# Transposing the last quarter's probabilities and the first gated rows by DMA in a two-layer decoder trunk

## The chip, the cores and the metric

The kernel runs on one core of a Trainium2 chip. The metric is device time in microseconds (us) of one execution; the time before is the median of three runs. A profile of one execution gives every instruction on the five engines with its start and length. PE (TensorE) multiplies matrices and writes PSUM, with a weight loader, PEld, beside it; DVE (VectorE), ACT (ScalarE) and POOL (GpSimd) work elementwise; SP (SyncE) issues the DMA transfers. Each engine, and SP's queue too, takes its instructions in a fixed order, and each instruction waits at the head of its queue until what it reads is there and what it overwrites is free.

## What is computed

The input is 256 tokens of width 1024. Layer 0 is a dilated attention mixer and layer 1 a forgetting attention mixer; each is followed by a gated feed-forward layer. All values are float32. Cut to what matters here:

```python
def dilated_mixer(h, w_in, w_out):                 # 3 groups (dilation 1, 4, 16), 16 heads of 64
    proj = (h @ w_in).reshape(B, S, N_GROUPS, 3, N_HEADS, HEAD_DIM)
    for g, (window, dil) in enumerate(DILATED_PATTERNS):
        ...
        o, lse = dilated_band_attention(q, k, v, dil, window // dil)
    wts = jax.nn.softmax(jnp.stack(lses, axis=0), axis=0)
    o = jnp.einsum('gbsh,gbshd->bshd', wts, jnp.stack(outs, axis=0))
    return o.reshape(B, S, ATTN_WIDTH) @ w_out

def swiglu(h, w_gu, w_down):                       # D_FF = 2816
    gu = h @ w_gu
    g, u = gu[..., :D_FF], gu[..., D_FF:]
    return (jax.nn.silu(g) * u) @ w_down

for i in range(2):
    h = h + (dilated_mixer, forgetting_mixer)[i](rmsnorm(h, ...), ...)
    h = h + swiglu(rmsnorm(h, ffn_norm[i]), ffn_w_gu[i], ffn_w_down[i])
return rmsnorm(h, final_norm)
```

## The kernel before

**Products in three parts.** Every large product is computed with its operands cut into a high part and a low part (`split`, L76: ACT copies the high part, L80, and DVE subtracts to get the low part, L84). One product is then three matmuls (`mm3`, L200, lines L203 and L208): high by high, high by low, low by high. In this text an *item* is one such group of three with an output of 512 columns.

**Weights.** They arrive in pieces of 128x2048, listed in use order in `order` (L141 to L149). `weights` (L154) issues each piece's two loads from SP into `raw` (five buffers) and cuts them on ACT and DVE into `wh` and `wl` (four buffers each, one pair per piece), up to two pieces ahead of the one that is used. In the feed-forward layer of the kernel before, the order is gu0, gu1, gu2, gu3, dn0, gu4, dn1, gu5, gu6, dn2 and so on: "gu" holds the gate and up columns of 128 hidden units, "dn" the down rows of 256.

**Mixer of layer 0.** The 16 heads are worked in four quarters, `hq` 0 to 3, each with two pairs of heads, `pr` 0 and 1. The 36 units of `a_units` are projections; attention steps are put behind units with `later(i, ...)`. A pair's probabilities are 128x640 per head, and the product with the values (`pv_a`, L534) needs them transposed in blocks of 128x128. There are two ways to transpose:

- Quarters 0 to 2 use `turn_a` (L519). A float32 is taken as two 16-bit halves. POOL copies the halves apart (L528), a transposing DMA issued from SP turns all ten 128x128 blocks of 16-bit values (L530, tile `turned`), and ACT joins the halves again (L531). The tiles lie in tag `pt` (three buffers) and tag `bias` (four buffers).
- Quarter 3 uses `trans_a` (L510): ten transposes on PE per pair into PSUM (`transposed`, L297, line L301), and copies out of PSUM (L306). Due at 38 and 39, with `pv_a` at 40, these run inside `out_proj`.

`values_12` (L274) moves the values of the two dilated groups into place with 16 POOL copies (L285). For quarter 3 they stand in the next-to-last unit.

**`out_proj`** (L658) multiplies the attention output `ot` (eight slices `k` of 128; slices 6 and 7 are the last quarter's) with four weight pieces, for token halves t = 0, 1 and column halves n = 0, 1. In layer 0 it does six items of t = 0 (n = 0, slices 0 to 5), the transposes of pair 0, three items, the transposes of pair 1, three items, `pv_a` for both pairs, and then the four items with slices 6 and 7. For t = 1 it does four items, then eight with `norm_t` of token half 0 behind them (L185: two normalisation passes on DVE, eight PE transposes at L196), and four more.

**Feed-forward layer** (`ffn`, L702). The first three gu pieces are computed in token-major layout, so that work can start before both token halves are normalised: gu0 and gu1 as a pair (`proj_pair`), gu2 by `proj_tok`. `gated` (L711) takes Silu on ACT (L714) and the product on DVE (L715). The results must be transposed before `down` can use them: four PE transposes for gu0 and gu1 (L775), two for gu2 (L784), each followed by `split` from PSUM. From gu3 on, `up` (L718) computes feature-major and needs no transposes; it uses one PSUM bank of tag `mm` (gate) and one of tag `tr` (up). `down(j, t)` (L733) adds piece dn j's product for token half t. The order is up(3), down(0), up(4), down(1), up(5), up(6), down(2) and so on. In layer 0 the result of gu2 itself lies in an `mm` bank, in layer 1 in an `o` bank. There are two banks per tag.

**Order of work.** The program text gives priorities; `first()` (L44) raises those of what it holds by 300, and `issue_after` ties an instruction behind another on its engine. The final order on each engine is fixed before the run.

Of the kernel before, what the change touches and what calls it, by code (L numbers as in the profile page):

```python
# [17 lines left out]
P = 128  # L18
# [14 lines left out]
def trunk(ctx: ExitStack, tc: tile.TileContext, T, out):  # L33
# [221 lines left out]

    def v_tile(o=None, r=None):

        v = ap.tile([P, 512], F32, tag="v", name="v", bufs=7)
        with first():
            if r:  # L260
                for t in range(2):
                    s = slice(t * S, (t + 1) * S)
                    nc.scalar.activation(v[:, s], o[:, s], AF.Copy, scale=r[t])
            elif o is not None:
                nc.scalar.activation(v, o, AF.Copy)
        return v
# [27 lines left out]

    copied = {}
# [214 lines left out]
    def trans_a(quad, pr):  # L510

        pt = quad["pt"]
        block = lambda h, i: pt[pr, h][:, i * P:(i + 1) * P]
        home = ("pt", "bias")[pr]
        quad["w", pr] = [transposed([block(h, 1 + qb) for h in range(2) for qb in range(2)], nc.scalar.copy, home=home),
                         transposed([block(h, 3) for h in range(2)], home=home),
                         transposed([block(h, b * 4) for h in range(2) for b in range(2)], nc.scalar.copy, "o", home)]

    def turn_a(quad, pr):  # L519

        quad["w", pr] = []
        bufs = {"pt": 3, "bias": 4}
        parts = lambda x: x[:, :640].bitcast(U16).rearrange("p (c t) -> p t c", t=2)
        for h in range(2):
            home = ("pt", "bias")[pr]
            w = ap.tile([P, 640 if home == "pt" else 6 * P], F32, tag=home, name="pt", bufs=bufs[home])
            split16 = w[:, :640].bitcast(U16)
            nc.gpsimd.tensor_copy(split16.rearrange("p (t c) -> p t c", t=2), parts(quad["pt"][pr, h]))  # L528
            turned = ap.tile([P, 6 * P], F32, tag="bias", name="turned", bufs=4)[:, :640].bitcast(U16)
            nc.sync.dma_start_transpose(turned.rearrange("p (g c) -> p g c", c=P), split16)  # L530
            nc.scalar.copy(parts(w), turned.rearrange("p (t c) -> p t c", t=2))  # L531
            quad["w", pr].append(w)

    def pv_a(quad, pr):  # L534
        vs, ws = quad["v"], quad["w", pr]
        o = psum("o")
        if len(ws) == 2:
            blocks = [w[:, :640].rearrange("p (i j) -> p i j", j=P) for w in ws]
            straight = lambda h: ws[h][:, P:3 * P]
            corner = lambda h: ws[h][:, 3 * P:4 * P]  # L540
            dilated = lambda h, a: blocks[h][:, 0:5:4, a * 32:a * 32 + 32]
        else:
            straight = lambda h: ws[0][:, h * S:(h + 1) * S]
            corner = lambda h: ws[1][:, h * P:(h + 1) * P]
            dilated = lambda h, a: halves(ws[2][:, h * S:(h + 1) * S], a)
        pv(o[:, :S], vs[0], 0, pr, straight, S, True, False)
        pv(o[:, P:S], vs[0], 1, pr, corner, P, False, False)
        halves = lambda x, a: x.rearrange("p (b n) -> p b n", b=2)[:, :, a * 32:a * 32 + 32]
        for a in range(4):
            pv(halves(o[:, :S], a), vs[1 + a % 2], a // 2, pr, lambda h: dilated(h, a), 64, False, a == 3)  # L550
# [6 lines left out]
    def later(i, fn, *a):  # L557
        due.setdefault(i, []).append((fn, a))

    quads = [{"hq": hq, "fm": {}, "pt": {}, "v": {}} for hq in range(4)]  # L560
    for i, (hq, g, w) in enumerate(a_units):
# [19 lines left out]
        if w < 2:  # L581
# [26 lines left out]
            if w == 1:  # L608
# [5 lines left out]
                if g == 2:  # L614
                    later(j + 1, scores_12, quad)
                    later(j + 1, softmax_a, quad)
                    for pr in range(2):
                        if hq == 3:
                            later(step(hq) + pr, trans_a, quad, pr)
                        else:  # L620
                            later(j + 1, turn_a, quad, pr)
# [36 lines left out]
    def out_proj(nm, ot, h, grow, ks, done, banks):  # L658
# [3 lines left out]
        res = []  # L662

        def part(t, acc, nk):
            last = None
            for n, k in nk:
                c = (k % 2) * D + n * 512
                last = mm3(acc[n], both(ot, ALL, k, slice(t * P, (t + 1) * P)),
# [3 lines left out]
        def cols(ks):  # L672
            return [(n, k) for n in range(2) for k in ks]

        for t in range(2):
            acc = [psum(banks[t]) for _ in range(2)]
            if t == 0:

                nk = cols(range(ks))
                last = part(t, acc, nk[:done])  # L680
                nk = nk[done:]
                per = -(-len(nk) // (len(due) - 1))
                for i in sorted(due):
                    with tc.issue_after(last.ins):
                        for fn, a in due[i]:
                            fn(*a)
                    last = part(t, acc, nk[:per]) or last
                    nk = nk[per:]
                due.clear()
                part(t, acc, nk)  # L690
                last = part(t, acc, cols(range(ks, KT)))
            else:
                part(t, acc, cols(range(2)))
                with tc.issue_after(last.ins):
                    part(t, acc, cols(range(2, 6)))
                    norm_t(*res[0], grow, xt, 0)
                    part(t, acc, cols(range(6, KT)))
            res.append(residual(acc, h[t], f"h_{nm}{t}"))
# [3 lines left out]
    def ffn(l, hs, xt, grow, mid):  # L702
# [54 lines left out]
        rows = {}  # L757
# [14 lines left out]
        tr = psum("tr")  # L772
        for f in range(2):
            for t in range(2):
                nc.tensor.transpose(tr[:, f * S + t * P:f * S + (t + 1) * P], rows[t][:, f, :], ident)  # L775
        act(0)
        split(acts[0], lambda y: y, tr)
# [4 lines left out]
        tr = psum("tr")  # L782
        for t in range(2):
            nc.tensor.transpose(tr[:, t * P:(t + 1) * P], a[:, t, :], ident)  # L784
# [26 lines left out]

    g_f = load_grow(1)
    hs, xt = out_proj("a_out", ot, x, g_f, 6, 6, ("sc", "mm"))
# [195 lines left out]
    hs, xt = out_proj("b_out", ot, [h for h, _ in hs], g_f, 6, 9, ("mm", "sc"))  # L1009
# [129 lines left out]
```

## Time and profile before

| | us |
|---|---|
| median of 3 runs | 737.42 (736.22 to 738.65) |
| the profiled execution's own time | 736.1 |
| its span, first to last instruction | 734.3 |
| around the span | 1.8 |
| weight and input bytes read | 136.00 MB, 187 GB/s over the span |
| granted TensorE clock, mean | 0.997 |

The page names busy time per engine, a picture of the span in 40 slices, the DMA queues, the chain of work that ended last, and the costliest groups of instructions. A matmul's listed length includes its pipeline, so that neighbours overlap: the time that one costs is the distance to the start of the next. Busy shares are means over stages with different limits; which wait counts is read from the timeline of a stage.

### The profile page before, as it was taken

How to read it: one execution, taken by the hardware profiler on the slowest of the kernel's cores; microseconds unless marked ns; L12 is line 12 of the kernel's file. 1: busy time of each engine (PE TensorE's matmuls, PEld its weight loads, DVE VectorE, ACT ScalarE, POOL GpSimd, SP SyncE). 2: the span in 40 equal slices, each digit the busy share in tenths (PEclk: the TensorE clock that was granted, in tenths of full speed). 3: DMA queues.
4: the chain of work that ended last, by engine and by line, in shares of the span. 5: the costliest groups of instructions: out<-in, count | busy, mean ns of one | idle time of the engine just before them, and what ended most of it. 6: DMA issues, size and time to landing. Idle time of an engine off the chain costs nothing.

```text
span 734.3 us, 14310 instructions
## 1 busy us (share of the span) xinstructions
PE 726.4 (99%) x5856; PEld 672.4 (92%) x5856; DVE 495.9 (68%) x762; ACT 388.7 (53%) x617; POOL 83.0 (11%) x118
## 2 busy tenths in 40 slices
PE   9999999999999999999999999999999999999996
PEld 7999989999988899999999989999889999999995
DVE  6997998998996775554555474576776554556533
ACT  7646747738445663444554453587475444545421
POOL 0600206007105000000000004110010000000001
PEclk9999999999999999999999999999999999999998
DMA  9865955956864376656567352874547656656601
GB/s 335 306 202 174 237 182 153 289 193 152 268 194 160 116 241 221 195 179 203 195 202 247 127 168 90 294 260 138 172 142 237 222 179 203 195 188 218 198 1 58
DMA packets 55042, 141.93 MB, mean 193 GB/s; under 512 B 20257, under 2 KB 21441, under 8 KB 54977
## 3 DMA queue, kind: packets, MB, share of 16 engines
q1 hardware_dynamic: 54832, 140.88, 59.4%
q8 instruction: 46, 0.75, 0.4%
q14 instruction: 20, 0.16, 0.1%
q10 hardware_dynamic: 144, 0.15, 0.1%
HBM read 136.00 MB, written 1.07 MB: 187 GB/s over the span
## 4 chain that ended last, share of the span: by engine, by line
PE 97%; DVE 1%; ACT 1%; POOL 0%; issue 0%; POOLq 0%; DVEq 0%; ACTq 0%
PE ps_mm L208 34%; PE ps_mm L203 17%; PE ps_tr L208 9%; PE ps_sc L208 8%; PE ps_o L208 7%; PE ps_tr L203 5%; PE ps_sc L203 4%; PE ps_o L203 4%; PE ps_o L313 2%; PE ps_sc L395 2%; PE ps_tr L196 1%; PE ps_tr L301 1%; PE ps_sc L476 1%; PE ps_o L322 1%; PE ps_sc L894 0%; PE ps_sc L458 0%
## 5 line engine op out<-in xcount | busy, mean ns | idle before, releaser
L80 ACT ACTIVATE wh<-raw 128x1024 fp32r<-128x1024 f32 x236 | 243.4, 1054 | 207.1 <-PE ps_tr L208 66.7
L84 DVE TENSOR_TENSOR wl<-raw,wh 128x1024 fp32r<-128x1024 f32 x236 | 288.3, 1242 | 82.6 <-ACT wh L80 82.4
L203 PE MATMUL ps_mm<-xt,wh 128*128 128x256 f32 x816 | 227.2, 279 | 0.2 <-ACT v L281 0.2
L208 PE MATMUL ps_mm<-xt,wl 128*128 128x256 f32 x816 | 226.0, 277 | 0.0
L208 PE MATMUL ps_mm<-xt,wh 128*128 128x256 f32 x816 | 226.0, 277 | 0.0
L203 PEld LDWEIGHTS ps_mm<-xt,wh 128*128 128x128 f32 x816 | 153.1, 188 | 2.2 <-issue 1.7
L208 PEld LDWEIGHTS ps_mm<-xt,wl 128*128 128x128 f32 x816 | 153.6, 188 | 0.1
L208 PEld LDWEIGHTS ps_mm<-xt,wh 128*128 128x128 f32 x816 | 153.4, 188 | 0.0
L208 PE MATMUL ps_tr<-xt,wh 128*128 128x256 f32 x304 | 83.9, 276 | 0.0
L208 PE MATMUL ps_tr<-xt,wl 128*128 128x256 f32 x304 | 83.9, 276 | 0.0
L203 PE MATMUL ps_tr<-xt,wh 128*128 128x256 f32 x304 | 83.7, 276 | 0.0
L730 DVE TENSOR_TENSOR sa<-ps_tr,sa 128x256 f32<-128x256 f32 x38 | 16.1, 424 | 73.5 <-PE ps_tr L208 73.5
L208 PEld LDWEIGHTS ps_tr<-xt,wh 128*128 128x128 f32 x304 | 57.1, 188 | 0.0
L208 PEld LDWEIGHTS ps_tr<-xt,wl 128*128 128x128 f32 x304 | 57.0, 188 | 0.0
L203 PEld LDWEIGHTS ps_tr<-xt,wh 128*128 128x128 f32 x304 | 57.0, 188 | 0.0
L203 PE MATMUL ps_mm<-wh,xt 128*128 128x512 f32 (+1 forms) x144 | 49.8, 346 | 0.0
L173 POOL TENSOR_SCALAR rs<-ssq 128x1 f32<-128x1 f32 x7 | 1.9, 271 | 420.6 <-ACT junk L182 420.6
L208 PE MATMUL ps_mm<-wl,xt 128*128 128x512 f32 (+1 forms) x149 | 49.1, 335 | 0.0
L208 PE MATMUL ps_mm<-wh,xt 128*128 128x512 f32 (+1 forms) x149 | 49.1, 335 | 0.0
L285 POOL COPY v<-v 32x256 f32<-32x256 f32 x64 | 40.5, 632 | 71.2 <-ACT v L281 68.6
L203 PE MATMUL ps_sc<-wh,ah 128*128 128x512 f32 x80 | 31.4, 392 | 0.0
L208 PE MATMUL ps_sc<-wl,ah 128*128 128x512 f32 (+1 forms) x82 | 31.3, 385 | 0.0
(232 smaller groups left out, 1113.6 us busy)
## 6 DMA issues: line engine op xcount, KB each, us to landing
raw<-in_gu SPq DMA_DIRECT2D x88, 512.0 KB, 4.8
raw<-in_a_in SPq DMA_DIRECT2D x68, 512.0 KB, 5.0
raw<-in_dn SPq DMA_DIRECT2D x44, 512.0 KB, 4.7
raw<-in_b_in SPq DMA_DIRECT2D x24, 512.0 KB, 5.0
raw<-in_a_out SPq DMA_DIRECT2D x8, 512.0 KB, 5.0
raw<-in_b_out SPq DMA_DIRECT2D x8, 512.0 KB, 4.4
bias<-sums SPq DMA_DIRECT2D x8, 384.0 KB, 6.6
grow<-in_norms SPq DMA_DIRECT2D x4, 512.0 KB, 5.7
```

The lines of the kernel that those rows point to most:

```text
L80: a = nc.scalar.activation(view(hi), src, AF.Copy)
L84: return nc.vector.tensor_tensor(view(lo), src, view(hi).bitcast(F32), op=ALU.subtract)
L196: nc.tensor.transpose(tr[:, k * P:(k + 1) * P], xn[:, kk * P:(kk + 1) * P], ident)
L203: nc.tensor.matmul(o, sh, mh, start=start, stop=False)
L208: last = nc.tensor.matmul(o[:, u], s, m[:, u], start=False, stop=end and u.stop == n)
L285: nc.gpsimd.tensor_copy(v[1 + a % 2][n:n + 32, a // 2 * S:a // 2 * S + S], by_t[a * 32:a * 32 + 32, t, g])
L301: nc.tensor.transpose(tr[:, i * P:(i + 1) * P], b, ident)
L313: nc.tensor.matmul(o[h * HD:(h + 1) * HD], v[:, c:c + HD], w(h), start=start, stop=stop)
L322: nc.tensor.matmul(o[:, :n], mhalf.to_broadcast([P, P]), mhalf.to_broadcast([P, n]), start=True, stop=True)
L395: nc.tensor.matmul(lead[t], xt[y][:, k, t * P:(t + 1) * P], w[z][:, u], start=k + y + z == 0, stop=k == KT - 1 and z == 1)
L476: nc.tensor.matmul(sc[h][c, o:o + 64], q[HR[h], pr, qb * P + a * 32:qb * P + a * 32 + 32], k[HR[h], pr].rearrange("p (b n) -> p b n", b=2) ...
L730: nc.vector.tensor_tensor(a, u, sg, op=ALU.mult)
```

## The change

- Quarter 3 uses `turn_a` too. Its 16-bit halves are copied apart on POOL for pair 0 and on DVE for pair 1, with raised priority. The joining copies are a function of their own, `join_a`, due at 38 (pair 0, on ACT, tied behind the last copy of the values) and at 39 (pair 1, on DVE). `trans_a` is gone.
- For pair 1, head 0, of every quarter the `turned` tile lies in tag `pt` and not in tag `bias`. In quarter 3 three `pt` and five `bias` tiles are used, with three and four buffers.
- `out_proj` takes a list of items `head` and places `at` which the due work stands. In layer 0 the list has 16 items: slices 0 to 3 of t = 0 (eight items), slices 0 and 1 of t = 1 (four), slices 4 and 5 of t = 0 (four). The joins stand behind items 4 and 9, `pv_a` behind item 16. The four items of t = 1 are therefore done before `pv_a`, and not after the residual of t = 0. In layer 1 the list and places give the order of before.
- In `ffn`, `gate` copies the halves of the gated rows apart (POOL for token half 0, DVE for token half 1); `turned` issues one transposing DMA and joins on ACT; `split` then reads SBUF. The third piece, gu2, goes the same way with POOL. The six PE transposes of each layer are gone.
- down(0) moves behind up(4), directly in front of down(1); the weight order becomes gu3, gu4, dn0, dn1, gu5.

```diff
-            order += [(f"gu{l}", f)] + ([(f"dn{l}", max(f // 2 - 1, 0))] if f == 3 or f % 2 == 0 and f > 3 else [])
+            order += [(f"gu{l}", f)] + [(f"dn{l}", 0)] * (f == 4) + [(f"dn{l}", f // 2 - 1)] * (f > 3 and f % 2 == 0)
...
-    def trans_a(quad, pr):
...
     def turn_a(quad, pr):
...
+        last = quad["hq"] == 3
+        by = (nc.gpsimd, nc.vector)[last and pr].tensor_copy
+        home = lambda tag: turn_tile(tag)[:, :640]
+        quad["w", pr], quad["turned", pr] = [], []
         for h in range(2):
...
+            with first() if last else nullcontext():
+                w = home(("pt", "bias")[pr])
+                apart = w.bitcast(U16)
+                by(apart.rearrange("p (t c) -> p t c", t=2), parted(quad["pt"][pr, h]))
+                turned = home(("bias", "pt")[pr * (h == 0)]).bitcast(U16)
+                nc.sync.dma_start_transpose(turned.rearrange("p (g c) -> p g c", c=P), apart)
             quad["w", pr].append(w)
+            quad["turned", pr].append(turned)
+            if not last:
+                join_a(quad, pr, h)
+
+    def join_a(quad, pr, h, by=nc.scalar.copy):
+        with tc.issue_after(copied["v"].ins) if quad["hq"] == 3 else nullcontext():
+            by(parted(quad["w", pr][h]), quad["turned", pr][h].rearrange("p (t c) -> p t c", t=2))
...
                     for pr in range(2):
-                        if hq == 3:
-                            later(step(hq) + pr, trans_a, quad, pr)
-                        else:
-                            later(j + 1, turn_a, quad, pr)
+                        later(j + 1, turn_a, quad, pr)
+                        for h in range(2) if hq == 3 else ():
+                            later(38 + pr, join_a, quad, pr, h, (nc.scalar.copy, nc.vector.tensor_copy)[pr])
...
+        cols = lambda t, ks: [(t, n, k) for n in range(2) for k in ks]
+        last = None
+        for a, b in zip((0, *at), (*at, len(head))):
+            last = part(head[a:b]) or last
+            if due:
+                with tc.issue_after(last.ins):
+                    for fn, a in due.pop(min(due)):
+                        fn(*a)
+        last = part(cols(0, range(KT)))
+        res = [residual(accs[0], h[0], f"h_{nm}0")]
+        part(cols(1, range(2)))
+        with tc.issue_after(last.ins):
+            part(cols(1, range(2, 6)))
+            norm_t(*res[0], grow, xt, 0)
+            part(cols(1, range(KT)))
+        res.append(residual(accs[1], h[1], f"h_{nm}1"))
...
+        rows = turn_tile("pt")[:, :512]
+        row16 = rows.bitcast(U16).rearrange("p (t f x c) -> p t f x c", t=2, f=2, x=2)
...
+        def turned(apart, by):
+            n = apart.shape[-1]
+            w = turn_tile("bias")[:, :n].bitcast(U16)
+            nc.sync.dma_start_transpose(w.rearrange("p (g c) -> p g c", c=P), apart.bitcast(U16))
+            by(parted(apart).rearrange("p x (f t c) -> p t f x c", t=2, c=P),
+               w.rearrange("p (t f x c) -> p t f x c", t=2, x=2, c=P))
 
         def gate(t):
             gu = pair[t].rearrange("p (a c b) -> p a c b", a=2, c=2)
-            rows[t] = gated(gu[:, :, 0, :], gu[:, :, 1, :], 2)
+            a = gated(gu[:, :, 0, :], gu[:, :, 1, :], 2)
+            with first():
+                (nc.gpsimd, nc.vector)[t].tensor_copy(row16[:, t], halves(a))
...
-        tr = psum("tr")
-        for f in range(2):
-            for t in range(2):
-                nc.tensor.transpose(tr[:, f * S + t * P:f * S + (t + 1) * P], rows[t][:, f, :], ident)
         act(0)
-        split(acts[0], lambda y: y, tr)
+        with first():
+            turned(rows, nc.scalar.copy)
+            split(acts[0], lambda y: y, rows)
         third = act(2)
         up(3)
         gu = o.rearrange("p (a c b) -> p a c b", a=2, c=2)
         a = gated(gu[:, :, 0, :], gu[:, :, 1, :], 2)
-        tr = psum("tr")
-        for t in range(2):
-            nc.tensor.transpose(tr[:, t * P:(t + 1) * P], a[:, t, :], ident)
-        split(*third, tr[:, :S])
-        for f in range(2, NF):
-            if f > 3:
-                up(f)
-            if f % 2 == 0:
-                j = f // 2 - 1
+        row = turn_tile("pt")[:, :S]
+        nc.gpsimd.tensor_copy(row.bitcast(U16).rearrange("p (t x c) -> p t x c", t=2, x=2), halves(a))
+        turned(row, nc.scalar.copy)
+        split(*third, row)
+        for f in range(4, NF):
+            up(f)
+            for j in {4: (0, 1)}.get(f, (f // 2 - 1,) if f % 2 == 0 else ()):
                 dn[j] = weights(f"dn{l}", j)
...
+    def blocks(t, ks):
+        return [(t, n, k) for i in ks for n in range(2) for k in (2 * i, 2 * i + 1)]
...
+    hs, xt = out_proj("a_out", ot, x, g_f, blocks(0, range(2)) + blocks(1, range(1)) + blocks(0, (2,)), (4, 9, 16),
+                      ("sc", "mm"))
...
+    hs, xt = out_proj("b_out", ot, [h for h, _ in hs], g_f, [(0, n, k) for n in range(2) for k in range(6)], (9, 12),
+                      ("mm", "sc"))
```

More of the change, by code (lines that the diff above doesn't have):

```diff
@@ L254, in p_tile @@
         return ap.tile([P, 640], dtype, tag="p", name=name, bufs=6)[:, :n]
+    copied = {}
     def v_tile(o=None, r=None):
@@ L508, in softmax_a, with parted @@
                         nc.vector.tensor_scalar(s, s, f, None, op0=ALU.mult)
-    def trans_a(quad, pr):
[L512 to L517, printed above, removed]
+    def parted(x):
+        return x.bitcast(U16).rearrange("p (c t) -> p t c", t=2)
@@ L519, in turn_a, with turn_tile @@
+    def turn_tile(tag):
+        return ap.tile([P, 640 if tag == "pt" else 6 * P], F32, tag=tag, name="pt", bufs={"pt": 3, "bias": 4}[tag])
     def turn_a(quad, pr):
-        quad["w", pr] = []
-        bufs = {"pt": 3, "bias": 4}
-        parts = lambda x: x[:, :640].bitcast(U16).rearrange("p (c t) -> p t c", t=2)
+        last = quad["hq"] == 3
+        by = (nc.gpsimd, nc.vector)[last and pr].tensor_copy
+        home = lambda tag: turn_tile(tag)[:, :640]
+        quad["w", pr], quad["turned", pr] = [], []
@@ L524, in turn_a @@
         for h in range(2):
[L525 to L530, printed above, removed]
@@ L536, in pv_a @@
         o = psum("o")
[L537 to L541, printed above, removed]
-        else:
[L543 to L547, printed above, removed]
+        blocks = [w.rearrange("p (i j) -> p i j", j=P) for w in ws]
+        pv(o[:, :S], vs[0], 0, pr, lambda h: ws[h][:, P:3 * P], S, True, False)
+        pv(o[:, P:S], vs[0], 1, pr, lambda h: ws[h][:, 3 * P:4 * P], P, False, False)
         halves = lambda x, a: x.rearrange("p (b n) -> p b n", b=2)[:, :, a * 32:a * 32 + 32]
         for a in range(4):
-            pv(halves(o[:, :S], a), vs[1 + a % 2], a // 2, pr, lambda h: dilated(h, a), 64, False, a == 3)
+            pv(halves(o[:, :S], a), vs[1 + a % 2], a // 2, pr, lambda h: blocks[h][:, 0:5:4, a * 32:a * 32 + 32],
+               64, False, a == 3)
         src = o[:, :S].rearrange("p (b a u) -> p b a u", b=2, a=4)
@@ L656, in residual, with out_proj, part @@
         return hn, parts
-    def out_proj(nm, ot, h, grow, ks, done, banks):
+    def out_proj(nm, ot, h, grow, head, at, banks):
         ws = [weights(nm, i) for i in range(4)]
         xt = xt_tile()
-        res = []
-        def part(t, acc, nk):
+        accs = {}
+        done = set()
+        def part(items):
             last = None
-            for n, k in nk:
+            for t, n, k in items:
+                if (t, n, k) in done:
+                    continue
+                done.add((t, n, k))
+                if t not in accs:
+                    accs[t] = [psum(banks[t]) for _ in range(2)]
@@ L667, in part @@
                 c = (k % 2) * D + n * 512
-                last = mm3(acc[n], both(ot, ALL, k, slice(t * P, (t + 1) * P)),
+                last = mm3(accs[t][n], both(ot, ALL, k, slice(t * P, (t + 1) * P)),
                            both(ws[k // 2], ALL, slice(c, c + 512)), k == 0, k == KT - 1)
             return last
-        def cols(ks):
-            return [(n, k) for n in range(2) for k in ks]
-        for t in range(2):
[L676 to L693, printed above, removed]
-                with tc.issue_after(last.ins):
[L695 to L698, printed above, removed]
@@ L756, in ffn, with halves @@
         pair = [psum(("o", "mm")[l]) for _ in range(2)]
-        rows = {}
+        rows = turn_tile("pt")[:, :512]
+        row16 = rows.bitcast(U16).rearrange("p (t f x c) -> p t f x c", t=2, f=2, x=2)
+        def halves(x):
+            return x.bitcast(U16).rearrange("p f (c x) -> p f x c", x=2)
+        def turned(apart, by):
[4 more added lines that the diff above has]
+               w.rearrange("p (t f x c) -> p t f x c", t=2, x=2, c=P))
         def gate(t):
             gu = pair[t].rearrange("p (a c b) -> p a c b", a=2, c=2)
-            rows[t] = gated(gu[:, :, 0, :], gu[:, :, 1, :], 2)
+            a = gated(gu[:, :, 0, :], gu[:, :, 1, :], 2)
+            with first():
+                (nc.gpsimd, nc.vector)[t].tensor_copy(row16[:, t], halves(a))
         for half in range(2):
@@ L1008, in trunk @@
     g_f = load_grow(3)
-    hs, xt = out_proj("b_out", ot, [h for h, _ in hs], g_f, 6, 9, ("mm", "sc"))
+    hs, xt = out_proj("b_out", ot, [h for h, _ in hs], g_f, [(0, n, k) for n in range(2) for k in range(6)], (9, 12),
+                      ("mm", "sc"))
     def finish(t, h, parts):
```

7 lines of the change are left out of this document (1 added, 6 removed).

## The prediction

> **What bounds the kernel now.** The page of the profile comes first: busy times, then the chain of work that ended last.
>
> ```profile
> PE 726.4 (99%) x5856; PEld 672.4 (92%) x5856; DVE 495.9 (68%) x762; ACT 388.7 (53%) x617; POOL 83.0 (11%) x118
> ...
> PE 97%; DVE 1%; ACT 1%; POOL 0%; issue 0%; POOLq 0%; DVEq 0%; ACTq 0%
> ```
>
> PE is busy for 726.4 of 734.3 us, and 97% of the chain that ended last lies on PE. So there are 8 us in which PE does not work, and two rules follow: an instruction taken from PE shortens the span by its distance to the next one, and work on the other four engines costs nothing until PE waits for it. The question is what leaves PE, and whether each result that now goes the longer way is there when PE asks.
>
> Next, the timeline of PE where the transposes stand (start, length, engine, line, tile). First the last quarter, inside `out_proj`:
>
> ```profile
> 225.52 0.40 PE L203 MATMUL ps_sc<-wh,oth 128*128 128x512 f32 x1
> ...
> 229.40 0.39 PE L208 MATMUL ps_sc<-wh,otl 128*128 128x512 f32 x1
> 229.63 0.81 PE L301 MATMUL ps_tr<-ident,p 128*128 128x128 f32 x6
> 230.29 0.60 PE L301 MATMUL ps_o<-ident,p 128*128 128x128 f32 x4
> 230.64 0.48 PE L203 MATMUL ps_sc<-wh,oth 128*128 128x512 f32 x1
> 230.96 0.40 PE L208 MATMUL ps_sc<-wl,oth 128*128 128x512 f32 x1
> ...
> 232.81 0.82 PE L301 MATMUL ps_tr<-ident,p 128*128 128x128 f32 x6
> ...
> 233.82 0.48 PE L203 MATMUL ps_sc<-wh,oth 128*128 128x512 f32 x1
> ...
> 236.09 2.45 PE L313 MATMUL ps_o<-pt,v 128*64 128x256 f32 x48
> ```
>
> Read starts, not lengths. Six items run from 225.52 to 229.63: 0.685 us each. The ten transposes hold PE from 229.63 to 230.64, 1.01 us, and the matmul behind them takes 0.32 to the next start, where an undisturbed one takes 0.23 (229.40 to 229.63): 0.09 more. The second ten are alike (232.81 to 233.82).
>
> Then the feed-forward layers, 0 above, 1 below:
>
> ```profile
> 270.86 0.28 PE L208 MATMUL ps_mm<-wh,xt 128*128 128x256 f32 x1
> 270.98 0.60 PE L775 MATMUL ps_tr<-ident,sa 128*128 128x128 f32 x4
> 271.34 0.36 PE L203 MATMUL ps_mm<-xt,wh 128*128 128x256 f32 x1
> 271.54 0.28 PE L208 MATMUL ps_mm<-xt,wh 128*128 128x256 f32 x1
> ...
> 277.07 0.38 PE L784 MATMUL ps_tr<-ident,sa 128*128 128x128 f32 x2
> 277.21 0.48 PE L203 MATMUL ps_sc<-wh,ah 128*128 128x512 f32 x1
> 277.53 0.40 PE L208 MATMUL ps_sc<-wl,ah 128*128 128x512 f32 x1
> ```
>
> ```profile
> 559.91 0.28 PE L203 MATMUL ps_o<-wh,xt 128*128 128x256 f32 x1
> ...
> 562.64 0.60 PE L775 MATMUL ps_tr<-ident,sa 128*128 128x128 f32 x4
> 563.00 0.36 PE L203 MATMUL ps_mm<-xt,wh 128*128 128x256 f32 x1
> ...
> 568.73 0.38 PE L784 MATMUL ps_tr<-ident,sa 128*128 128x128 f32 x2
> 568.87 0.48 PE L203 MATMUL ps_sc<-wh,ah 128*128 128x512 f32 x1
> ```
>
> **The change part by part: what leaves PE.** Last quarter: 2 x (1.01 + 0.09) = 2.20 us. Each feed-forward layer: four transposes 0.36 plus 0.08 behind them (0.20 against 0.12), two transposes 0.14 plus 0.09 (0.32 against 0.23), 0.67 in all; two layers 1.34. Sum: 3.54 us. Items, ups, downs and the products with the values keep their number and shape, so their reordering alone adds nothing.
>
> **What is added.** The same route is in the trace for quarters 0 to 2, by line: count, then shortest, median and longest in ns.
>
> ```profile
> L528 POOL COPY pt<-p x12: 1247/1358/2245, 72.2 to 183.4; 128x1280 uint16<-128x1280 uint16 x12
> ...
> L530 SPq DMA_TRANSPOSE turned<-pt x12: 1267/1366/1601, 73.8 to 185.0; - x12
> ...
> L531 ACT COPY pt<-turned x12: 1647/1672/1698, 77.5 to 188.5; 128x1280 uint16<-128x1280 uint16 x12
> ...
> DMA to landing us min/median/max: 3.3/3.5/5.8
> ```
>
> One turn is 1.36 on POOL, 3.5 (3.3 to 5.8) from issue to landing, of which SP is held 1.37, and 1.67 on ACT. The DVE forms are new. By the scaling rows below, 0.435 for 320 float32 on average, 1280 halves cost 0.87 if counted as 640 words and 1.74 if counted singly; I take 1.36, POOL's time for the same shape, which lies between.
>
> *Last quarter.* Its surroundings on POOL, DVE and SP:
>
> ```profile
> 219.69 11.84 POOL L285 COPY v<-v 32x256 f32<-32x256 f32 x16 [33.33 <-ACT v L281]
> ...
> 221.89 1.74 DVE L508 TENSOR_SCALAR p<-p,c 128x256 f32<-128x256 f32 x4
> 223.74 1.74 DVE L508 TENSOR_SCALAR p<-p,c 128x256 f32<-128x256 f32 x4
> 225.41 5.41 DVE L84 TENSOR_TENSOR wl<-raw,wh 128x1024 fp32r<-128x1024 f32 x4
> ...
> 221.79 9.38 SPq L101 DMA_DIRECT2D raw<-in_gu  x5
> ```
>
> PE asks for pair 0 behind 16 items: 225.52 + 16 x 0.685 = 236.5, and for pair 1 half of the products later, 237.7. Supply: head 0's probabilities are scaled at 222.8. POOL is amid its value copies (0.74 each), of which four would be done; the raised priority should let the turn in at 223.4. POOL ends at 224.8 and 226.1; transfers land at 228.3 and 229.6; ACT joins by 230.0 and 231.7: 4.8 us in hand. Pair 1's copies on DVE end at 226.8 and 228.2. The fourth transfer takes the fifth `bias` tile of four, so it waits for the first join: 230.0, landing 233.5, DVE join 234.9: 2.8 us in hand. Queued behind that transfer on SP are gu loads; the five in the row spread to 231.2 anyway, and their weights are first multiplied in the feed-forward layer, over 15 us later. Behind the joins on ACT stand weight cuts for the same layer. Behind DVE's two copies stand the four cuts of 225.41: done at 233.5 instead of 230.8, while the slices that need their first half come behind item 12, 233.7, and the rest behind `pv_a`. POOL's remaining value copies end at 234.3 instead of 231.5, before 236.5. I cost all this at nothing; uncovered, each microsecond behind those times is one of PE's.
>
> *Four items of t = 1 go ahead of `pv_a`.* That takes them from behind the residual of t = 0:
>
> ```profile
> 241.86 0.69 DVE L654 TENSOR_TENSOR h_a_out<-ps_sc,x 128x512 f32<-128x512 f32 x1 [0.69 <-PE ps_sc L208]
> ...
> 244.40 1.42 DVE L191 SCALAR_TENSOR_TENSOR xn<-h_a_out,rs,grow 128x512 f32<-128x512 f32 x2 [0.69 <-POOL rs L176]
> ```
>
> The norm ends 245.82 - 241.86 = 4.0 us after the last item of t = 0; its transposes had 12 items (8.2 us) of cover and now have eight (5.5): 1.5 us in hand, cost nothing. Piece a_out 0 is free sooner, so gu0's cuts may start sooner; a cut in the way of the last quarter's split could cost one instruction, at most 1.35 on DVE (5.41 / 4); I take nothing.
>
> *Feed-forward layers.*
>
> ```profile
> 269.01 0.42 DVE L715 TENSOR_TENSOR sa<-ps_o,sa 128x256 f32<-128x256 f32 x1
> ...
> 273.42 0.68 DVE L84 TENSOR_TENSOR al<-ps_tr,ah 128x512 fp32r<-128x512 f32 x1
> ...
> 275.57 0.42 DVE L715 TENSOR_TENSOR sa<-ps_mm,sa 128x256 f32<-128x256 f32 x1
> ```
>
> ```profile
> 272.15 0.58 ACT L80 ACTIVATE ah<-ps_tr 128x512 fp32r<-128x512 f32 x1
> ...
> 274.73 0.38 ACT L714 ACTIVATE sa<-ps_mm 128x256 f32<-128x256 f32 x1
> ```
>
> Gated rows of half 1 are ready at 269.4. DVE copy of 512 halves (0.4 x 1.36) 270.0; landing 273.5; join of 1024 halves (0.8 x 1.67) 274.8; high part 275.4; low part 276.1, or 278.4 with the slowest landing. down(0) now stands behind two ups of 5.73 (271.34 to 277.07): 282.4. In hand: 6.3 or 4.0. gu2's rows are ready at 276.0; POOL 276.5, landing 280.0, join (0.4 x 1.67) 280.7, split within 1.3: 282.0, against down(1) at 282.4 + 8 x 0.685 = 287.9. The transfers hold SP about 1.4 us per layer more or less twice, against gu and dn loads that now have a down more of lead. Cost: nothing. One new tightness: in layer 0 gu2's result lies in an `mm` bank, which up(4) needs right behind up(3), at 276.7; it is free at 276.0. In layer 1 it lies elsewhere.
>
> One unknown: in layer 1 the 24 matmuls from 559.91 to 562.64 step 0.114, but the 48 from 563.00 to 568.73, behind the transposes, 0.118 without the first's 0.08. If that goes with the transposes, 0.2 us per layer more is gained; if it lasts into up(4), as much is lost: 0.4 either way, and I take zero.
>
> **Sum.** 736.1 - 3.54 = 732.6 against the profiled execution. That execution lies 1.3 below the median; from the median, 737.42 - 3.54 = 733.9. Its own range is 733.0 to 735.2.
>
> **The rivals.**
>
> *A, slower: the turn stands behind all 16 value copies on POOL.* POOL's order is fixed beforehand, and values are ready before probabilities. Then pair 0's copies start at 231.5 and end at 232.9 and 234.3, transfers land at 236.4 and 237.8, joins end at 238.1 and 239.8; the fourth transfer waits for the first join, lands at 241.6, joined at 243.0: 5.3 late. With the slowest landing on both legs, 9.8. Net +1.8 to +6.3, midway 741.4. It decides at 3.5 us of lateness. For it: quarter 3's probabilities come 3 us behind the first value copy. Against: the priority, and that eight value copies ahead (225.6) cost nothing yet. [...]
>
> *B: the chain of the fourth transfer is a little late.* Slow landings on both legs give 230.6, 232.3, 238.1, 239.4: 1.7 late; twelve value copies ahead (228.6) give 2.4. Time 735.6 to 736.3.
>
> *C: up(4) of layer 0 waits for its bank.* If ACT's join, with raised priority and a slow landing (275.8), stands ahead of gu2's Silu, it is 277.1, 277.7, 278.1, and behind DVE's low part (278.4) the product ends at 278.8: 2.1 late, 736.0. For: Silu ran at 274.73, late, though its bank was complete at 271. Against: the median landing gives 276.5.
>
> *D: nothing comes off the end,* because PE was not the bound. The 99% speak against it; it gets no chance of its own.
>
> **How the numbers follow.** Forecast 0.60, A 0.10, B 0.14, C 0.10; 0.06 for other losses or gains, such as the step of the matmuls, four of these faster. 0.3% is 2.2 us, about what a measurement of this kernel can tell from no change. Faster: 0.60 + 0.04 = 0.64; within: B and C, 0.24; slower: 0.12. The three runs of before spread by 1.2 either way, so the range goes from 732.4 to 737.4: it holds forecast, B and C and leaves out A.
>
> **What would show it.** PE's busy time 3.5 us lower, no L301 transposes before 250 us and none in `ffn`; the products with the values starting about 0.4 us later than 236.09, with no gap before either pair (else A or B; POOL's order decides); no gap before up(4) of layer 0 (else C), before down(0), or before the norm's transposes. A gap at one of these places whose length makes up the difference would prove the forecast wrong there.

## The result: slower, and the profile after

Eleven runs of each kernel give 741.07 us for the changed kernel (737.82 to 743.80) and 736.38 us for the kernel before (735.03 to 738.65). The ratio is 1.006, with an interval of 1.0044 to 1.0075: **slower by 0.6%, 4.7 us**, where 733.9 us was forecast. (The forecast was reckoned from the median of the first three runs of before, 737.42; from the median of all eleven the same sum gives 732.8.) The profiled execution after is the longest of the eleven, 743.8 us with a span of 742.0, so the lengths below add up to more than the medians do: its span is 7.7 us over that of the profiled execution before.

The page after, busy times and chain:

```profile
PE 727.9 (98%) x5824; PEld 671.4 (90%) x5824; DVE 504.1 (68%) x766; ACT 393.2 (53%) x619; POOL 91.9 (12%) x124
...
PE 86%; DVE 6%; DMA 3%; ACT 2%; issue 1%; SPq 0%; POOL 0%; POOLq 0%; DVEq 0%; ACTq 0%
```

PE has 32 instructions fewer, as it should: 20 transposes in the last quarter, 6 in each feed-forward layer. Yet its busy time did not fall by 3.5 us but rose by 1.5, and the chain now spends 14% of the span off PE where it spent 3%. Two questions follow: what PE waits for, and why its remaining matmuls take longer.

The waits of PE (engine, tile, line, releaser: total, times, longest):

```profile
PE ps_o L313 <- DVE pt L536: 2.2, 1, 2.2
PE ps_mm L203 <- ACT sa L719: 2.0, 1, 2.0
...
PE ps_mm L203 <- DVE qk L443: 0.6, 1, 0.6
```

None of the three is there before. The waits left out last 0.3 to 0.9 us, and the longest of them, 0.9 at L322, is in the profile before as well. The first of the three is pair 1's product with the values, the second up(4) of layer 0, the third a place nobody looked at, in quarter 0. The timeline of PE around the first:

```profile
237.77 1.76 PE L313 MATMUL ps_o<-pt,v 128*64 128x256 f32 x26
241.71 1.33 PE L313 MATMUL ps_o<-pt,v 128*64 128x256 f32 x22 [2.17 <-DVE pt L536]
242.97 0.80 PE L203 MATMUL ps_sc<-wh,oth 128*128 128x512 f32 x1
243.56 0.63 PE L208 MATMUL ps_sc<-wl,oth 128*128 128x512 f32 x1
244.47 0.79 PE L208 MATMUL ps_sc<-wh,otl 128*128 128x512 f32 x1 [0.27 <-DVE otl L84]
...
249.32 0.60 PE L208 MATMUL ps_mm<-wl,oth 128*128 128x512 f32 x1
249.75 0.40 PE L208 MATMUL ps_mm<-wh,otl 128*128 128x512 f32 x1
```

Read the starts again: after the gap the matmuls follow each other at 0.43 us where the undisturbed ones step by 0.23, until 249.75. The table of stretches (length; busy time and count of PE, PEld, DVE, ACT, POOL; granted clock, DMA share, GB/s) names the reason, here and behind the second gap:

```profile
244.50:250.00 5.50, 5.50 (x14) 4.30 (x15) 1.81 (x3) 0.78 (x3) 0.23 (x1) 0.52 0.47 161
283.60:287.40 3.80, 3.71 (x18) 3.71 (x19) 3.16 (x6) 3.14 (x6) 0.61 (x1) 0.55 0.84 322
```

PE works almost without a break at a mean granted clock of 0.52 and 0.55. The trace's record of the clock is sharper than these means: exactly 0.50 for 6.83 us from 242.93 and for 3.41 us from 283.89, and 1.00 otherwise, from 4.00, where the record begins, until PE's work ends. So a gap is paid twice here: while PE waits and again while it runs at half speed. Half of 6.83 and of 3.41 us is 5.1 us, and PE's busy time came out 5.0 above the forecast (1.5 more instead of 3.5 less).

By stages, from the starts of the same matmuls in both timelines (us):

| stage | before | after | difference |
|---|---|---|---|
| to the last quarter's scores | 213.06 | 214.06 | +1.00 |
| from there to the norm's transposes | 36.77 | 40.74 | +3.97 |
| feed-forward layer 0, to the norm behind it | 184.45 | 187.55 | +3.10 |
| mixer of layer 1 | 107.31 | 107.39 | +0.08 |
| feed-forward layer 1 | 185.64 | 185.19 | -0.45 |

With 2.20 and 0.67 us taken from PE, the row of the last quarter hides a loss of 6.2 us and that of layer 0 one of 3.8. Waits and half speed account for most of it: 2.2 + 0.3 + 3.4 us in the last quarter (0.3 is a wait for `otl`), 2.0 + 1.7 in layer 0. The first row can't be read as quarter 0's step: 0.77 of its 1.00 us has arisen before quarter 0's scores (63.45 against 64.22), and from there to the last quarter's scores profiles of kernels that are alike in this stretch differ by 1.5 us (148.1 to 149.6, before and the four versions of the last experiment).

### Why the fourth transfer was late

The timelines of POOL and SP in the changed kernel, around the last quarter's turn:

```profile
220.39 5.14 POOL L287 COPY v<-v 32x256 f32<-32x256 f32 x9 [31.86 <-ACT v L283]
225.59 2.57 POOL L526 COPY pt<-p 128x1280 uint16<-128x1280 uint16 x2
...
226.87 3.44 SPq L528 DMA_TRANSPOSE pt<-pt  x2
230.41 0.65 SPq L101 DMA_DIRECT2D raw<-in_gu  x1
231.16 1.35 SPq L528 DMA_TRANSPOSE pt<-pt  x1
232.60 1.54 SPq L101 DMA_DIRECT2D raw<-in_gu  x2
234.25 1.49 SPq L528 DMA_TRANSPOSE pt<-pt  x1
```

Nine value copies went ahead of the turn on POOL, not four (and not 16, as rival A had it). On SP two gu loads stand between the third and the fourth transfer; the prediction had them behind it. The copies of ACT and DVE that join, and the landings of these four transfers:

```profile
231.31 3.16 ACT L536 COPY pt<-pt 128x1280 uint16<-128x1280 uint16 x2 [1.62 <-DMA pt<-pt]
...
240.78 0.88 DVE L536 COPY pt<-pt 128x1280 uint16<-128x1280 uint16 x1 [3.38 <-DMA pt<-pt]
...
DMA to landing us min/median/max: 4.2/4.8/6.4
```

The last join ends at 241.7, not at 234.9. The 6.8 us are 2.9 for the first of the two joins on ACT (done at 232.9 instead of 230.0: POOL 2.1, its landing 0.9 longer, its copy 0.1 shorter), 1.4 for the two loads issued ahead of the transfer, 2.9 for its own landing (6.4 instead of 3.5), less 0.4 for a DVE copy shorter than reckoned.

### Why up(4) waited

PE, then ACT, then two pieces of the chain that ended last:

```profile
281.37 0.28 PE L208 MATMUL ps_tr<-xt,wl 128*128 128x256 f32 x1
283.69 0.42 PE L203 MATMUL ps_mm<-xt,wh 128*128 128x256 f32 x1 [2.04 <-ACT sa L719]
...
282.07 1.33 ACT L758 COPY pt<-pt 128x1024 uint16<-128x1024 uint16 x1 [4.03 <-DMA pt<-pt]
283.27 0.36 ACT L719 ACTIVATE sa<-ps_mm 128x256 f32<-128x256 f32 x1
...
284.06 0.37 ACT L705 ACTIVATE sa<-ps_mm 128x256 f32<-128x256 f32 x1
```

```profile
234.25 6.44 DMA pt<-pt
...
274.89 7.08 DMA pt<-pt
```

The transfer of the gated rows lands after 7.1 us. ACT stands at the join for the last 4.03 us of that, and behind the join wait up(3)'s Silu (L719) and gu2's (L705). PE starts when the former has read its bank.

### Quarter 0

DVE's two cuts for the next weight piece, and POOL's fourth copy of quarter 0's turn, before and after:

```profile
77.31 2.35 DVE L84 TENSOR_TENSOR wl<-raw,wh 128x1024 fp32r<-128x1024 f32 x2
...
79.21 1.56 POOL L528 COPY pt<-p 128x1280 uint16<-128x1280 uint16 x1 [2.64 <-ACT pt L531]
```

```profile
78.07 3.40 DVE L84 TENSOR_TENSOR wl<-raw,wh 128x1024 fp32r<-128x1024 f32 x2
...
77.61 1.65 POOL L526 COPY pt<-p 128x1280 uint16<-128x1280 uint16 x1 [0.27 <-DVE p L508]
```

Before, POOL waited 2.64 us for a free tile, and its copy fell behind DVE's cuts. With the `turned` tile moved to `pt` it runs at once, beside the first cut, and the two take 3.40 us instead of 2.35. Listed singly, the first takes 2.27 us and the second, which starts after POOL's copy has ended, 1.21. A step of PE's matmuls at 82 us is then 0.88 instead of 0.11.

### The profile page after: what moved, and what is told of

Its sections match the earlier page's. It is cut to its first block, busy times and chain, and to the rows that moved or that the text cites. A ratio compares the mean times of both kernels' runs of the same rounds, so it can differ in the third digit from the quotient of the medians.

```text
span 742.0 us, 14276 instructions
## 1 busy us (share of the span) xinstructions
PE 727.9 (98%) x5824; PEld 671.4 (90%) x5824; DVE 504.1 (68%) x766; ACT 393.2 (53%) x619; POOL 91.9 (12%) x124
## 4 chain that ended last, share of the span: by engine, by line
PE 86%; DVE 6%; DMA 3%; ACT 2%; issue 1%; SPq 0%; POOL 0%; POOLq 0%; DVEq 0%; ACTq 0%
PE ps_mm L208 30%; PE ps_mm L203 15%; PE ps_tr L208 9%; PE ps_sc L208 8%; PE ps_o L208 7%; PE ps_tr L203 5%; PE ps_sc L203 4%; PE ps_o L203 4%; DVE wl L84 2%; DMA pt<-pt 2%; PE ps_o L313 1%; DMA otl<-in_lead 1%; PE ps_tr L196 1%; ACT wh L80 1%; DMA raw<-in_a_in 1%
## 5 line engine op out<-in xcount | busy, mean ns | idle before, releaser
L84 DVE TENSOR_TENSOR wl<-raw,wh 128x1024 fp32r<-128x1024 f32 x236 | 292.1, 1258 | 77.1 <-ACT wh L80 76.9
L287 POOL COPY v<-v 32x256 f32<-32x256 f32 x64 | 43.1, 674 | 73.0 <-ACT v L283 70.3
L208 PE MATMUL ps_sc<-wh,al 128*128 128x512 f32 (+1 forms) x82 | 31.2, 385 | 0.0
```

What stands on the lines that cost most here:

```text
L84: return nc.vector.tensor_tensor(view(lo), src, view(hi).bitcast(F32), op=ALU.subtract)
L208: last = nc.tensor.matmul(o[:, u], s, m[:, u], start=False, stop=end and u.stop == n)
L287: nc.gpsimd.tensor_copy(v[1 + a % 2][n:n + 32, a // 2 * S:a // 2 * S + S], by_t[a * 32:a * 32 + 32, t, g])
```

## The experiments

The theory after reading the traces: PE's saving is real, and it is lost to three waits, two of them made dearer by the clock behind them (no slow clock follows the one in quarter 0). The expectations call two rivals *order*, that the new order of downs and weight pieces costs the time, and *traffic*, that the added transfers and copies slow PE all along. A third is that the clock falls for another reason than the gap. Each time below is a median, with the median of the kernel before in the same set of runs (735.93 for the first four; 735.45 for the next two and for 1 and 4 copies in the last experiment; 735.49 for the rest).

### The last quarter's part alone

```diff
-        rows = turn_tile("pt")[:, :512]
...
+        rows = {}
...
+        tr = psum("tr")
+        for f in range(2):
+            for t in range(2):
+                nc.tensor.transpose(tr[:, f * S + t * P:f * S + (t + 1) * P], rows[t][:, f, :], ident)
         act(0)
...
+        split(acts[0], lambda y: y, tr)
```

The feed-forward layers, and the weight order with them, are those of before.

> Quarter 3 and out_proj as changed, the feed-forward layers as before. Waits (theory: PE waits 2.2 us for pair 1's join, then runs at a granted clock of 0.5 to 0.8 for some 8 us): the 2.2 us of transposes are saved, some 2 of wait, 3 to 4 of slow clock and 0.8 of a wait in quarter 0 are paid, 738.5 to 740 against 736.4 before. Order (rival: the moved downs and weight order cost the time): 734 to 735, since no down is moved here. Traffic (rival: more transfers and copies slow PE all along): about 738, with no gap at the products of pair 1 needed for it.

741.49 us, ratio 1.008 (1.0067 to 1.0093), +5.6 us: worse than expected, and as slow as the whole change. Part of it lies outside the span: in three of the five runs the time is 2.1 to 3.0 us over the span, where 1.8 is usual. By the medians of the spans it is 739.0 against 734.1, +4.9. Its wait:

```profile
PE ps_o L313 <- DVE pt L536: 3.8, 1, 3.8
```

The same two loads stand ahead of its fourth transfer, which lands after 7.5 us. Slow steps follow (mean clock 0.62 from 242.6 to 247.1). No down is moved in this version, so *order*, which expected 734 to 735, doesn't explain it. Nor is the new order of `out_proj`'s items as such to blame: later versions keep it and are faster.

### The feed-forward part alone

```diff
+    def trans_a(quad, pr):
...
+                        if hq == 3:
+                            later(step(hq) + pr, trans_a, quad, pr)
+                        else:
+                            later(j + 1, turn_a, quad, pr)
...
-    hs, xt = out_proj("a_out", ot, x, g_f, blocks(0, range(2)) + blocks(1, range(1)) + blocks(0, (2,)), (4, 9, 16),
+    hs, xt = out_proj("a_out", ot, x, g_f, [(0, n, k) for n in range(2) for k in range(6)], (6, 9, 12),
```

> Feed-forward layers as changed, quarter 3 and out_proj as before. Waits: 1.34 us of transposes saved, 2.2 of wait at up(4) of layer 0 and 1.7 of slow clock behind it paid; 738 to 739.5, layer 1 shorter by 0.4 to 0.7. Order: both layers longer by the same amount, about 741. Traffic: both layers a little longer, about 738.5.

735.94 us, ratio 1.0 (0.999 to 1.0009): no change, better than expected. The wait of up(4) is there, but 0.9 us long, and no slow steps follow it (0.11 to 0.12 us from the second matmul on):

```profile
277.39 0.38 PE L203 MATMUL ps_mm<-xt,wh 128*128 128x256 f32 x1 [0.90 <-ACT sa L729]
277.61 0.28 PE L208 MATMUL ps_mm<-xt,wh 128*128 128x256 f32 x1
```

Layer 0 costs 0.4 us more than before, layer 1 gives 0.45 back. Neither *order* (741 expected) nor *traffic* (738.5) shows. Here the gated rows' transfer landed after 5.9 us, not 7.1. So this part's cost isn't fixed: in the whole change the same wait is 2.0 us long, with the slow clock behind it. And its price here was not proportional to its length: with the 0.67 us saved, layer 0 lost 1.1 us with the wait of 0.9, and 3.8 with that of 2.0.

### The join behind gu2's Silu

```diff
+        gu = o.rearrange("p (a c b) -> p a c b", a=2, c=2)
+        with first():
+            a = gated(gu[:, :, 0, :], gu[:, :, 1, :], 2)
         act(0)
         with first():
-            turned(rows, nc.scalar.copy)
-            split(acts[0], lambda y: y, rows)
+            with tc.issue_after(behind_silu[0].ins):
+                turned(rows, nc.scalar.copy)
+            split(acts[0], lambda y: y, rows, after=behind_silu[1])
```

gu2's Silu and product are made first; the join and the low part are tied behind them.

> The changed kernel with gu2's Silu and product ahead of the joining copy of the gated rows on ACT and of the low part on DVE. Waits: the gap at up(4) of layer 0 goes with its slow clock, 3 to 4 us less than the changed kernel: 737 to 738. Order and traffic: unchanged, 741.

738.25 us, ratio 1.0039 (1.0025 to 1.0052), +2.3 us where the changed kernel has +4.7; *order* and *traffic* expected 741. up(4)'s matmuls step by 0.12 without a gap; the waits of pair 1 (2.9 us in its profile) and of quarter 0 remain. This shows rival C's mechanism: the place of the join on ACT made PE wait.

### All four gu loads behind the fourth transfer

```diff
-            nc.sync.dma_start(raw, T[key[0]][key[1]][:, u])
+            with tc.issue_after(copied["turn"].ins) if key[0] == "gu0" and key[1] < 2 else nullcontext():
+                nc.sync.dma_start(raw, T[key[0]][key[1]][:, u])
...
-                nc.sync.dma_start_transpose(turned.rearrange("p (g c) -> p g c", c=P), apart)
+                copied["turn"] = nc.sync.dma_start_transpose(turned.rearrange("p (g c) -> p g c", c=P), apart)
```

The edit is made to the changed kernel, without the one above.

> The changed kernel with the first four gu loads issued behind quarter 3's fourth transposing transfer. Waits: that transfer is issued near 233 and lands within 3.5 to 4.5 us, the gap at pair 1's products goes with its slow clock, 5 to 6 us less than the changed kernel: 735 to 736. If the wait for the fifth bias tile and not the loads makes it late, half of it stays: 738 to 739. Order and traffic: unchanged, 741.

740.58 us, ratio 1.0065 (1.0053 to 1.0078): a miss. The number is the one that *order* and *traffic* expected (741), but the trace shows another reason. SP, the landings of the four transfers, ACT and PE:

```profile
227.29 6.97 SPq L529 DMA_TRANSPOSE pt<-pt  x4
...
DMA to landing us min/median/max: 3.4/3.6/3.8
...
239.74 2.23 ACT L80 ACTIVATE wh<-raw 128x1024 fp32r<-128x1024 f32 x2 [4.73 <-DMA raw<-in_gu]
241.87 1.07 ACT L80 ACTIVATE oth<-ps_o 128x256 fp32r<-128x256 f32 x2
...
237.94 2.45 PE L314 MATMUL ps_o<-pt,v 128*64 128x256 f32 x48
242.53 0.50 PE L204 MATMUL ps_sc<-wh,oth 128*128 128x512 f32 x1 [2.15 <-ACT oth L80]
```

The transfers do what was expected: with no load among them all four land within 3.8 us, and the 48 products run without a gap. But gu0's cut stands on ACT ahead of the last quarter's own split (`oth`), and now it waits for its load. The wait moved by one consumer and kept its length, 2.15 us, and the slow steps stand behind it too (mean clock 0.58 from 243 to 247). The wait of up(4) is there as well, 2.2 us, but no slow steps follow it, and layer 0's loss is 2.3 us where the changed kernel's is 3.8.

### Only the second piece's loads behind it, with the Silu first

```diff
+            with tc.issue_after(copied["turn"].ins) if key == ("gu0", 1) else nullcontext():
```

> The changed kernel with gu2's Silu ahead of the join, and with only the two loads of piece gu1 issued behind quarter 3's fourth transposing transfer; piece gu0 keeps its place, so its cut on ACT is not late for the last quarter's split. Waits: the fourth transfer lands by 237.5 and PE has no gap at pair 1's products, at the four items behind them or at up(4); what is left is the 0.9 us at 82 us: 734 to 735, 1.0 to 1.9 under before. If lateness only moves to another consumer again, as with all four loads held: 737 to 738, with a new gap between 238 and 246.

734.41 us, ratio 0.9987 (0.9978 to 0.9996): 1.0 us under the kernel before. SP's fourth transfer, and DVE's join for it:

```profile
233.44 2.95 SPq L529 DMA_TRANSPOSE pt<-pt  x1
...
238.46 0.91 DVE L537 COPY pt<-pt 128x1280 uint16<-128x1280 uint16 x1 [0.18 <-DMA pt<-pt]
```

With only the third transfer in front of it, it is issued 0.8 us earlier than in the changed kernel and lands at 238.4, 5.0 us later instead of 6.4. Left are, above all, quarter 0's step and 0.8 us in which PE waits for `otl` (L84).

### Quarter 0 to 2 as before, too

```diff
-                turned = home(("bias", "pt")[pr * (h == 0)]).bitcast(U16)
+                turned = home(("bias", "pt")[last * pr * (h == 0)]).bitcast(U16)
```

> As silu_hold, and in quarters 0 to 2 all turned tiles stay in tag bias as before the change. Waits: the 0.9 us gap at 82 us goes as well: 733 to 734, 2.2 to 3.2 under before, the 3.5 of the transposes less what new slow stretches take. Traffic (added transfers and copies cost PE all along): no better than 735.5.

733.50 us, ratio 0.9972 (0.9962 to 0.9982). POOL's fourth copy is back at 80.00, and DVE's two cuts have their length of before:

```profile
78.09 2.35 DVE L84 TENSOR_TENSOR wl<-raw,wh 128x1024 fp32r<-128x1024 f32 x2
```

The step at 82 us is gone, and 0.9 us with it (from -1.0 to -1.95 against before). *Traffic* expected no better than 735.5: the added transfers are all still there, so they aren't the main cost.

### The last wait removed as well

```diff
-        split(ot, lambda x: x[:, kt, :].rearrange("p (b u a) -> p b a u", a=4, b=2), src)
+        copied["low"] = split(ot, lambda x: x[:, kt, :].rearrange("p (b u a) -> p b a u", a=4, b=2), src)[1]
...
-        ws = [weights(f"gu{l}", f) for f in range(2)]
+        ws = [weights(f"gu{l}", f, None if l else copied["low"]) for f in range(2)]
```

The low parts of the first gu pieces are tied on DVE behind the last quarter's split; the gu pieces are also asked for later in the program.

> As all_fix, and the low parts of gu0's and the next gu pieces are tied behind the last quarter's split on DVE. Waits: the 0.7 us gap left at 240 us in all_fix goes: 732.5 to 733.2, about 2.5 to 3 under before. If DVE's cuts then come late for the feed-forward layer: 733.5 or more, with a gap after 250.

732.59 us (731.91 to 732.91), ratio 0.996 (0.9948 to 0.9972): **2.9 us faster than before, faster than both kernels**. All the waits of PE that are left, both also in the profile before (0.9 and 0.2):

```profile
PE ps_o L323 <- DVE mhalf L66: 0.9, 1, 0.9
PE ps_mm L204 <- ACT v L284: 0.3, 1, 0.3
```

By stages of the profile, against before: last quarter and `out_proj` 34.48 us (-2.29), feed-forward layer 0 183.56 (-0.89), layer 1 185.19 (-0.45): 3.63 together, where 3.54 were forecast. The medians show 2.9 of it.

### What a gap costs by itself

Four versions of the kernel before, in which PE must wait in front of up(8) of layer 0: a transpose whose result nobody uses reads a tile that POOL copies 1, 4, 8 or 13 times first.

```diff
+            if (l, f) == (0, 8):
+                late = ap.tile([P, 640], F32, tag="pt", name="late", bufs=3)[:, :S]
+                nc.gpsimd.tensor_copy(late, acts["a"])
+                for _ in range(3):
+                    nc.gpsimd.tensor_copy(late, late)
+                held = nc.tensor.transpose(psum("tr")[:, :P], late[:, :P], ident)
+            with tc.issue_after(held.ins) if (l, f) == (0, 8) else nullcontext():
```

> The kernel before, with one PE transpose put in front of up(8) of layer 0, which reads a POOL copy of up(7)'s result: PE waits about 1.2 us there and nothing else changes. If a wait costs only itself: 1.2 to 1.5 us over before. If the granted clock falls behind any wait: 3 us or more.

> As gap_short with four POOL copies in a row, so that PE waits some 3 us. If a wait costs only itself: 3 to 3.5 us over before. If the granted clock falls behind a wait of over 2 us, as the traces with gaps suggest: 5 to 7 us over before, with 0.5 to 0.8 of the clock for 4 to 8 us behind the gap.

> As gap_long with eight POOL copies, PE waits some 3 us in the middle of layer 0. If a wait costs only itself: 3.0 to 3.5 over before. If the granted clock falls behind waits of over 2 us: 5 or more over before, and the steps of the matmuls behind the gap are 1.3 to 2 times as long for some us.

> As gap_long with 13 POOL copies, PE waits some 5 us. If a wait costs only itself: 5 to 5.5 over before. If the granted clock falls behind waits of over 2 us: 7.5 or more over before.

| copies | wait in its profile (1 copy: of the weight loader), us | that profile's layer 0 over 184.45 | median, us | over before | ratio |
|---|---|---|---|---|---|
| 1 | 0.3 | +0.2 | 735.96 | +0.5 | 1.0 (0.999 to 1.0011) |
| 4 | 1.0 | +1.6 | 737.98 | +2.5 | 1.0028 (1.0019 to 1.0038) |
| 8 | 2.3 | +3.3 | 740.55 | +5.1 | 1.0067 (1.0055 to 1.0078) |
| 13 | 2.9 | +5.3 | 741.40 | +5.9 | 1.0093 (1.0079 to 1.0107) |

The waits came out shorter than meant, since PE did other matmuls meanwhile and a POOL copy took only 0.4 to 0.7 us (3.25 us of POOL for nine with 13 copies, 3.99 for six with eight). So the times can't be held against the expectations, which were for 1.2, 3, 3 and 5 us. A wait of 1 us or more cost 1.4 to 1.8 times its listed length in the profiled runs, and 2 to 2.5 times by the medians, whose own waits aren't known. PE behind the longest wait:

```profile
323.79 0.48 PE L793 MATMUL ps_tr<-ident,late 128*128 128x128 f32 x1 [2.94 <-POOL late L792]
...
325.99 0.41 PE L203 MATMUL ps_mm<-xt,wh 128*128 128x256 f32 x1
...
326.74 0.28 PE L208 MATMUL ps_mm<-xt,wh 128*128 128x256 f32 x1
```

Steps of 0.21 at a clock of 0.50 until 326.4, then 0.11 again: here the clock fell behind a gap with no transposing transfer near. In the profiles with four and eight copies there are no slow steps; the run with eight was the fastest of its six (739.03, 3.5 us up). So the falling clock explains the worst cases (the last section has them), and part of the extra cost of the shorter waits stays unexplained.

## Why the prediction was wrong, step by step

**What leaves PE** was right: 3.54 us forecast, 3.63 in the stages of the best version, where nothing new is waited for. That the sum came out this close is partly luck, for the feed-forward layers gave 0.89 and 0.45 where 0.67 each was forecast. The prediction's "one unknown", put at zero, accounts for both. In layer 0 of the best version up(3)'s 48 matmuls step by 0.113 us, 0.118 before, and up(4)'s are unchanged: 0.2 us gained. In layer 1 up(3) keeps 0.118, and up(4) goes from 0.114 to 0.118: 0.2 us lost. What sets the step isn't shown. (The "own range" of 733.0 to 735.2 doesn't follow from the three runs either: less 3.54 they give 732.7 to 735.1.)

**"The fourth transfer ... 2.8 us in hand" failed.** Each link was reckoned at a median and the order on POOL and SP was guessed. The loads that "queued behind that transfer on SP" stood ahead of it, and the landing of 6.4 us lies outside the 3.3 to 5.8 that the trace of before shows. Rival B named this chain, with a lateness of 1.7 to 2.4; it became 2.2 us of wait in the profile, 2.9 and 3.8 in two others. It had no term for the loads in front.

**"One new tightness"** was the other failed cover. Rival C, at 0.10, had the place and the mechanism: a slow landing, and the join ahead of Silu on ACT. That 2.0 us of wait came out where 2.1 was given is partly luck: the landing was 7.1 where C took 5.8, and PE waited for another bank, freed earlier in the chain, by up(3)'s Silu right behind the join. The transfer was issued about as far ahead of up(4) as forecast (6.6 us, by the prediction 6.7); its landing, 7.1 us against 3.5, was the step that failed.

**B and C were set as alternatives; both came.** They share a cause, transfers that landed late behind loads (after 6.4 and 7.1 us), so their chances weren't independent. Added up, they alone would have given no change.

**A gap was priced at its own length.** This is the term missing from every rival: behind both waits PE ran at a granted clock of 0.50. In the last quarter 6.2 us were lost with 2.2 of listed wait, in layer 0 3.8 with 2.0; 3.4 and 1.7 of that are the slow clock.

**Quarter 0 wasn't in the sum at all.** Moving `turned` to `pt` removed a wait on POOL, and the copy that came earlier slowed DVE. Undoing it was worth 0.9 us.

**Rival A** did not occur, as the nine value copies show; that its 741.4 lies next to the measured 741.07 is chance. The cover of down(0), down(1) and the norm's transposes held: no PE wait is listed there. The DVE copies were 0.98 and 0.88, near the lower bound of 0.87, not the 1.36 taken; that helped, and changed nothing.

## What to carry to other kernels

Work moved from the bound engine to a DMA is free only if it is there in time, so take each queue's order as unknown until seen, and reckon a transfer that stands behind loads at its slowest landing (here 6.4 to 7.5 us). When a wait is removed by holding something back, look at who is next in a fixed order: holding all the loads moved the gap by one consumer, holding two of the four removed it. A gap of two microseconds or more on the matrix engine cost 1.0 to 1.4 times its listed length in the profiles where the clock stayed up, and 1.5 to 2.8 times where it fell: price it with the clock, and try first to have none.

## What was not expected of the hardware

**The clock fell behind short gaps.** Six waits of 2.0 to 3.8 us were followed by a granted clock of 0.50, for 3.4 us five times and for 6.8 once; behind 0.9 and 1.0 us (the feed-forward part alone, four copies) the clock stayed up, and so it did behind 2.2 (up(4) with all four loads held) and 2.3 (eight copies). In the two traces of before and after, the record of the clock begins 6.39 and 4.00 us into the span, and from there all its changes lie whole multiples of 3.413 us apart (212 before; 70, 2, 10, 1 and 132 after). Cut into stretches of this length, counted from where the record begins, the changed kernel's profile has PE idle for 0.64 and 0.60 of the stretch right ahead of the two slow ones, and for at most 0.14 of any other until PE's work ends; before, no stretch has more than 0.05, and the clock stays at 1.00. With 13 copies PE was idle for 0.68 of the stretch ahead of the slow one. For the other three cases about 0.7 is an estimate, from the starts of PE's matmuls around the gap and the end of the slow steps. With eight copies, where the clock stayed up, the gap lay across two stretches, and PE was idle for 0.48 of the first. The stretch of the gap and the one behind it, first the changed kernel's gap of 2.2 us, then eight copies, then 13 (columns as above: the second number is the length, the third PE's busy time, the clock stands third from the end):

```profile
239.52:242.93 3.41, 1.24 (x23) 1.12 (x22) 2.15 (x3) 0.26 (x1) 0.00 (x0) 1.00 0.60 189
242.93:246.35 3.42, 3.15 (x9) 2.00 (x8) 2.00 (x3) 0.65 (x1) 0.00 (x0) 0.50 0.58 186
...
317.24:320.66 3.42, 1.79 (x7) 0.83 (x5) 2.40 (x3) 0.29 (x1) 3.17 (x5) 1.00 0.48 156
320.66:324.07 3.41, 2.71 (x24) 2.72 (x25) 0.00 (x0) 0.00 (x0) 0.58 (x2) 1.00 0.47 162
...
319.77:323.18 3.41, 1.09 (x5) 0.56 (x3) 0.01 (x1) 0.00 (x0) 2.98 (x8) 1.00 0.72 229
323.18:326.59 3.41, 2.80 (x13) 2.80 (x14) 0.00 (x0) 0.00 (x0) 0.50 (x2) 0.50 0.06 24
```

So a gap of 2.0 us came with a slow clock and one of 2.3 us without. The changed kernel's own runs differ as well: the three with a mean clock of 0.997 or more took 737.8 to 739.0 us, the other eight 738.8 to 743.8. What makes the clock fall, and why one slow stretch was 6.8 us long, isn't shown.

**The transposing transfers landed later with loads among them.** The last quarter's four transfers of 128x1280 landed in 3.4 to 3.8 us with no load issued among them (all four loads held), in at most 5.2 and 5.4 with one (the best version, two loads held), and the fourth in 6.4 and 7.5 with two loads right before it on SP (the whole change, the last quarter's part alone).

**A DVE cut took longer beside a POOL copy.** DVE's cut with two operands took 2.27 us beside POOL's 16-bit copy and 1.21 behind it (quarter 0 of the changed kernel). With that copy back behind both cuts, the two took 2.35 us together.
